# Add and GELU, 1024 x 4096 floats: another map from HBM rows to partitions

## The chip, the cores and the metric

The kernel runs on one core of one Trainium2 chip. The metric is the device time of the program in microseconds (us). A profiled execution gives a span, from the first to the last instruction, and its own device time, which is a little longer than the span.

## The reference

Two inputs of 1024 x 4096 float32 (16 MiB each), one output of the same size. Every element stands alone:

```python
def reference(x, y):
    z = x + y
    return (0.5 * z * (1 + np.tanh(np.sqrt(2 / np.pi) * (z + 0.044715 * z ** 3)))).astype(np.float32)
```

Since no element depends on another, any part of the flat arrays may sit in any partition, as long as x, y and the output use the same map.

## The kernel before

The 4,194,304 elements are dealt over 128 partitions, 32,768 to each (TOT), in two halves of 16,384 (HALF, 64 KB per partition). SBUF holds all of z (128 x 32,768, which receives x, then the sum, then the result) and one half of y, which is loaded twice into the same tile. One helper, `rows` (L91), says which bytes of HBM belong to columns lo to hi of all partitions; every load and store goes through it.

The transfers are few and large. SyncE issues all seven in this order (the list `sp`): y's columns 0 to 703 and 704 to 16,383 of the first half (`load_y`, L144), both halves of x (`load_x`, L139), the second half of y (L144), and the two halves of the output (`store`, L148). The first two issues are moved to the front of the program by `begin_early`; the last store's completion is waited for by ScalarE instead of SyncE (`wait_late`).

The compute is cut into 20 chunks of 512 to 2048 columns. A chunk is added on VectorE or on GpSimd (`add`, L159), in eight chunks with x copied to PSUM by ScalarE before (`copy`, L152), and then ScalarE applies the GELU in place (`gelu`, L171). Three lists written out by hand (`on_vector`, `on_gpsimd`, `on_scalar`) give each engine its order.

What waits for what: the adds of a half wait for both loads of it; y's second half is loaded into the tile of the first, so its issue waits until the first half's adds are through; a store waits for the GELUs of its half. All seven transfers run on one queue, spread over 16 DMA engines, in order of issue. A DMA engine moves one contiguous piece of one partition as one packet: 64 KB, or 2,816 and 62,720 B for the two pieces of y's first half.

Before the change, `rows` cuts the flat array into two blocks of 8 MB, one for each half, and deals each block to the 128 partitions in 64 KB rows: partition p has the row at p x 64 KB. Eight neighbouring partitions are 512 KB, and groups of eight follow each other at 512 KB.

## Time and profile before

| what | value |
|---|---|
| median of 3 runs | 120.17 us (120.12 to 120.42) |
| profiled execution | 120.31 us |
| its span | 118.8 us |
| DVE, ACT, POOL busy | 29.1, 44.1, 13.8 us |
| DMA packets | 1008, 50.33 MB |
| mean rate over the span | 424 GB/s |

The page gives shares of the span and groups of instructions; the DMA issues have a line each with the time from issue to landing. A landing counts from the issue, so it holds the wait behind earlier transfers of the same queue too. The trace also has a record for every DMA packet, with its start, its duration and its size. Of the 1008 packets 896 carry data, seven times 128; the other 112 are the few bytes that tell a semaphore that an engine is through with its part of a transfer.

### The profile page before, as it was taken

To read this page: it belongs to the slowest core of one execution; us is meant where nothing else is said; L and a number is where in the kernel's file an instruction comes from. 1 tells how busy PE (TensorE), PEld (TensorE's weight loads), DVE (VectorE), ACT (ScalarE), POOL (GpSimd) and SP (SyncE) were. 2 spreads that over 40 slices of the span, in tenths; PEclk is the share of its full clock that TensorE was granted. 3 is DMA by queue.
4 is the path that set the end of the run, shared out by engine and by line. 5 is a ranking of instruction groups with operands and counts; after the bars stand their busy time and mean duration, and the time that the engine had idled before them with its cause. 6 is when DMAs were issued, how large, how long until landed. Compare 5 with 4: busy or idle time off the path is not lost.

```text
span 118.8 us, 115 instructions
## 1 busy us (share of the span) xinstructions
DVE 29.1 (24%) x18; ACT 44.1 (37%) x30; POOL 13.8 (12%) x7
## 2 busy tenths in 40 slices
DVE  0000000000000099994000000009999930000000
ACT  4000000000000096893049999903799990000000
POOL 0000000000000019980000000009500000000000
DMA  9779977998889988998899888998899888988891
GB/s 459 338 338 422 591 338 338 507 552 353 353 353 662 397 353 353 574 485 353 353 441 618 353 353 353 640 419 353 353 552 507 353 353 353 706 353 353 353 640 66
DMA packets 1008, 50.33 MB, mean 424 GB/s; under 512 B 112, under 2 KB 112, under 8 KB 240
## 3 DMA queue, kind: packets, MB, share of 16 engines
q1 hardware_dynamic: 1008, 50.33, 98.5%
HBM read 33.55 MB, written 16.78 MB: 424 GB/s over the span
## 4 chain that ended last, share of the span: by engine, by line
DMA 55%; DVE 14%; ACT 10%; DVEq 1%; ACTq 0%; issue 0%; SPq 0%
DMA z<-in_x_dram 34%; DMA y<-in_y_dram 21%; DVE z L159 14%; ACT z L171 10%; DVEq L214 1%; ACTq L214 0%; DVEq L159 0%; SPq L144 0%
## 5 line engine op out<-in xcount | busy, mean ns | idle before, releaser
L171 ACT ACTIVATE z<-z 128x2048 f32<-128x2048 f32 (+3 forms) x20 | 29.7, 1555 | 5.4 <-DVE z L159 5.4
L152 ACT COPY ps<-z 128x2048 f32<-128x2048 f32 (+2 forms) x8 | 13.0, 1654 | 47.0 <-DMA z<-in_x_dram 45.3
L159 DVE TENSOR_TENSOR z<-z,y 128x2048 f32<-128x2048 f32 (+2 forms) x9 | 13.6, 1571 | 40.2 <-DMA z<-in_x_dram 40.2
L159 DVE TENSOR_TENSOR z<-ps,y 128x2048 f32<-128x2048 f32 (+2 forms) x8 | 15.6, 2014 | 25.3 <-DMA y<-in_y_dram 25.3
L159 POOL TENSOR_TENSOR z<-z,y 128x2048 f32<-128x2048 f32 x3 | 13.5, 4533 | 70.8 <-DVE z L159 43.6
L199 ACT ACT_TABLE_LOAD x1 | 1.3, 1283 | 1.3 <-PEq L231 1.3
L198 DVE MEMSET one<- 128x1 f32 x1 | 0.1, 59 | 1.3 <-PEq L231 1.3
L199 ACT ACTIVATE one<-one 128x1 f32<-128x1 f32 x1 | 0.2, 202 | 0.0
L231 POOL MEMSET const-float32-0.0<- 128x1 f32 x1 | 0.1, 99 | 0.2 <-issue 0.2
L231 POOL MEMSET const-bfloat16-1.0<- 128x1 bf16 x1 | 0.1, 102 | 0.0
L231 POOL MEMSET const-uint8-127<- 128x1 uint8 x1 | 0.1, 102 | 0.0
L231 POOL MEMSET const-float32-1.0<- 128x1 f32 x1 | 0.1, 99 | 0.0
## 6 DMA issues: line engine op xcount, KB each, us to landing
y<-in_y_dram SPq DMA_DIRECT2D x1, 7840.0 KB, 21.7
y<-in_y_dram SPq DMA_DIRECT2D x1, 352.0 KB, 3.0
z<-in_x_dram SPq DMA_DIRECT2D x2, 49.7
out_dram<-z SPq DMA_DIRECT2D x2, 21.6
y<-in_y_dram SPq DMA_DIRECT2D x1, 25.1
```

What stands on the lines that cost most here:

```text
L152: nc.scalar.copy(out=in_psum(c), in_=zt[:, a:b])
L159: ins = eng.tensor_add(out=zt[:, a:b], in0=first, in1=yt[:, o : o + b - a])
L171: nc.scalar.activation(out=zt[:, a:b], in_=zt[:, a:b], func=act.Gelu_apprx_tanh)
L198: nc.vector.memset(one[:, :1], 0.0)
L199: nc.scalar.activation(out=one[:, :1], in_=one[:, :1], func=act.Gelu_apprx_tanh)
L214: tc.compile()
L231: nc = _bacc.Bacc("TRN2", target_bir_lowering=False, num_devices=1)
```

## The change

`rows` takes another map. The flat array is cut into 16 parts of 1 MB (`q`). Each part is cut into two halves of 512 KB (`h`), and each of these into eight rows of 64 KB (`j`). Partition 8 q + j has, for half h, row j of half h of part q. So a group of eight partitions still has 512 KB in one piece for each half, but the groups lie 1 MB apart, and the two halves of the data alternate in HBM every 512 KB instead of filling 8 MB each. The view of the HBM side that a transfer gets has two counts (16, 8) and the columns instead of one count (128) and the columns; the SBUF side is not touched. Nothing else is changed.

```diff
-    blocks = [(0, HALF), (HALF, TOT)]
+    Q = 16
 
     def rows(array, lo, hi):
-        flat, at = array.rearrange("n d -> (n d)"), 0
-        for f, e in blocks:
-            if f <= lo and hi <= e:
-                own = flat[P * at : P * (at + e - f)].rearrange("(p c) -> p c", p=P)
-                return own[:, lo - f : hi - f]
-            at += e - f
-        raise AssertionError((lo, hi))
+        h = lo // HALF
+        assert hi <= (h + 1) * HALF
+        own = array.rearrange("n d -> (n d)").rearrange("(q h j c) -> h q j c", q=Q, h=2, j=P // Q)
+        return own[h][:, :, lo - h * HALF : hi - h * HALF]
```

## The prediction

> **What bounds the kernel now.** I read the page first, then the chain of waits, then SyncE's own waits, then the records of the single DMA packets. From the page, the busy time of the engines, the DMA queue and the DMA issues:

> ```profile
> span 118.8 us, 115 instructions
> DVE 29.1 (24%) x18; ACT 44.1 (37%) x30; POOL 13.8 (12%) x7
> q1 hardware_dynamic: 1008, 50.33, 98.5%
> HBM read 33.55 MB, written 16.78 MB: 424 GB/s over the span
> ...
> y<-in_y_dram SPq DMA_DIRECT2D x1, 7840.0 KB, 21.7
> y<-in_y_dram SPq DMA_DIRECT2D x1, 352.0 KB, 3.0
> z<-in_x_dram SPq DMA_DIRECT2D x2, 49.7
> out_dram<-z SPq DMA_DIRECT2D x2, 21.6
> y<-in_y_dram SPq DMA_DIRECT2D x1, 25.1
> ```

> No compute engine is busy for more than 37% of the span, and the one DMA queue fills its 16 engines for 98.5% of it: the kernel is a train of transfers. The chain that ended last, in order of time:

> ```profile
> 1.25 40.22 DMA z<-in_x_dram
> ...
> 41.60 13.36 DVE z L159 x7
> 54.96 0.02 SPq L144
> ...
> 55.02 25.12 DMA y<-in_y_dram
> ...
> 84.85 11.86 ACT z L171 x7
> ```

> It names DVE and ACT too, but the DMA engines work on meanwhile: the load of y's second half is issued at 55.02 while x's second half is still moving. SyncE's own waits say who holds an issue back:

> ```profile
> SPq L144 <- DVE z L159: 52.0, 1, 52.0
> SPq L148 <- ACT z L171: 41.9, 2, 21.9
> ```

> These waits cost little as long as an issue comes before the engines run dry, so I compared issues with packets. The trace holds 896 data packets, seven times 128 (one for each partition and transfer). Grouped by transfer (us from the span's start; ns of one packet; excess is the time above the fastest packet, per engine):

> ```
> transfer          issue   first packet  last ends   min   mean   max  excess
> y cols 0-703       0.00       1.03         2.63      109  151.5   769   340
> y cols 704-16383   0.42       2.25        21.84     2314 2371.7  2593   461
> x half 0           1.25      21.20        41.16     2418 2418.3  2422     2
> x half 1           1.63      40.54        60.48     2418 2418.8  2432     6
> y half 1          55.02      59.87        79.80     2418 2418.3  2431     3
> out half 0        77.33      79.20        99.11     2418 2418.0  2420     0
> out half 1        97.77      98.63       118.43     2418 2420.0  2456    16
> ```

> A 65,536 B packet takes 2,418 ns, 27.1 GB/s on one engine, and does so almost without exception in x, in the second y half and in both stores, reads and writes alike. That is the pace of a DMA engine alone with its packets, not that of a crowded memory. Time above it is paid in the first 22 us only: the small first packets (up to 769 ns against 109) and the long y rows, whose mean by row within an engine runs 2408, 2329, 2365, 2429, 2464, 2350, 2315, 2314 ns. In the course of that load the starts of the 16 engines' packets spread from 0.38 to 0.64 us, and from then on they keep to 2,418 ns. I read this as streams that begin nearly in step, get in each other's way, and push one another apart until they no longer do.

> The floor follows. Per engine 8 x 0.109 + 8 x 2.314 + 40 x 2.418 = 116.1 us of packets at their fastest; with the first packet at 1.03 us and 0.4 us from the last packet's end (118.43) to the span's end it is 117.5 us. The remaining 1.3 us are the excess above (0.340 + 0.461 + 0.03 = 0.83 us per engine) and 0.5 us from engines that start late (between 1.03 and 1.56 us).

> **The change part by part.** No instruction is added or removed and none moves past another: seven DMA issues, 18 DVE, 30 ACT and 7 POOL instructions stay, in the same order, with the same waits. Every partition still holds 16,384 consecutive values of each half; only which 64 KB of HBM they are differs, and reads and the store use the same map, so the arithmetic is the same. Compute and the waits in the table: 0.

> *Bytes and packets.* In the code the last dimension stays contiguous, 65,536 B (2,816 and 62,720 B for y's first half). Seven times 128 packets stay, sum 0.

> *The issue.* The HBM side is now described with two counts (16 and 8) instead of one (128). An issue takes SyncE 328 to 424 ns now (L144), and two of them lie open: the first, which nothing covers (the second y issue follows it, but its first packet waits for the 352 KB ahead of it until 2.25 us), and out half 1, issued at 97.77 where the first engine runs dry at 98.52 and the next packet starts at 98.63, so 0.11 us of idle are there already. The others are early by at least 1.9 us (out half 0: 77.33 against 79.20), the two x issues by 20 and 39 us. The trace shows no issue with two counts. Bounds: 0, and the spread of the issues that are there, 0.1 us, for each of the two, 0.2 us together. I take 0.05 us, near nothing, since the number of packets that has to be written is unchanged.

> *The addresses.* This is the change. If an engine takes eight neighbouring partitions, 16 streams which stood 512 KB apart, all 8 MB in a row, now stand 1 MB apart over the whole 16 MB. In the settled 97 us (x half 0 to out half 1, 40 packets an engine) the price of an address is at most 16 ns per eight packets. With the fastest packets already equal to the mean, nothing can be gained there. In the first 22 us between 0 and all of the 0.80 us excess can be gained (0.340 + 0.461), or it can grow. Bound above: if it doubles, +0.80 us. If the worst row of the y load (2464 against 2314 ns, 6.5%) held for all 48 long packets of an engine, 48 x 2.4 x 0.065 = +7.5 us. I take 0: the settled rows, which are nine tenths of the train, are the nearest, and whether a start in step at 1 MB apart collides more or less than at 512 KB no row tells.

> [...]

> **Sum.** 118.8 + 0.05 + 0 = 118.85 us of span. The profiled run took 120.31 us, 1.51 around its span, and lies 0.14 above the median of 120.17. Against the median: 120.2 us, no change. A difference of 0.3% (0.36 us) is about what a measurement of this kernel can tell from none.

> **Rivals.**

> *The start collides less (faster).* For: the only excess in the train stands there, it depends on which addresses are touched together, and spacing is what changes. Against: the small packets' excess may be the first access after a pause (the first of each engine averages 374 ns, the second 159, the third 119), which no address cures. Half of the 0.80 us, with the 0.5 us of late starts untouched, gives 119.8; all of it 119.4. I name 119.6.

> *The start collides more (slower).* The mechanism: all 16 streams begin within half a microsecond of each other at addresses that differ only in bits above 1 MB instead of 512 KB; if fewer of them tell the memory's parts apart, more streams meet, and they need longer to spread. Place: the y load in the first 22 us, perhaps once more in the first row of out half 1, where eight engines start together (2434 ns). Price: the excess doubles, +0.8, so 121.0. It decides from +0.36 us, that is when the mean y packet rises above 2,417 ns (2,371.7 + 360/8). For: row five of that load is worse than row one, so the streams do not simply drift apart. Against: from 17 us on (row seven) they are clear of each other.

> *The streams never clear (much slower).* Same place, but the collisions stay for all 48 long packets: 127.7 at the worst row's 6.5%. Against it stands that equal streams, once apart, keep their distance, as they do for 97 us now. [...]

> *The split over the engines changes.* SBUF still counts 128 partitions, HBM now 16 x 8. If the two are dealt to the engines differently than before, so that two engines share what one had, or only eight engines get work, the six halves of 19.35 us (x half 0 lands at 41.45, out half 1 at 118.8, four steps between) double: about 235 us. For: no transfer of this form is in the trace. Against: both 128 and 16 deal evenly over 16 engines.

> **How the numbers follow.** No change (within 0.3%) 0.38, start better 0.28, start worse 0.22, never clear 0.08, split 0.04. The likeliest is 120.2 and its own range is 119.85 to 120.55. To leave out no more than 2 in 10 the range takes in both cases of the start: its low end is 119.2, since all of the excess and a part of the late starts is the most that can go; its high end is 122.0, an excess that more than triples at the start. The last two cases, 0.12 together, stay outside. A case near the bound can fall on its other side, so: faster 0.30, same 0.35, slower 0.35.

> **What would show it.** Right: x, y half 1 and out packets still at 2,418 ns, 128 for each transfer, first packet at 1.0 to 1.1 us, and the landings 19.35 us apart from 22 us on. Faster by the start: x half 0's first packet before 20.9 us (now 21.20), all else shifted by as much. Slower by the start: the same packet after 21.6 us. Never clear: packets above 2,418 ns in x and the stores, landings more than 19.4 us apart. A changed split: other packet counts at a time, DMA share far under 98%. The forecast is wrong most easily by the start, whose 0.8 us is more than twice the bound.

## The result, and the profile after

The changed kernel takes 238.22 us (median of 5 runs, 238.05 to 239.96) against 120.17 us before: a ratio of 1.9857, 95% interval 1.9781 to 1.9934. Its profiled execution took 238.05 us with a span of 236.5 us, 117.7 us more than before.

The page of the changed kernel: busy time, the DMA share and rate in 40 slices of the span, the queue, and the issues with their time to landing.

```profile
span 236.5 us, 115 instructions
DVE 29.1 (12%) x18; ACT 44.1 (19%) x30; POOL 13.7 (6%) x7
...
DMA  9897889988889988889988889985989889998993
GB/s 231 170 339 170 170 170 203 321 177 177 177 177 211 321 177 177 177 177 244 288 177 177 177 177 266 266 177 211 321 177 355 177 177 244 199 244 222 211 211 89
...
q1 hardware_dynamic: 1008, 50.33, 98.8%
HBM read 33.55 MB, written 16.78 MB: 213 GB/s over the span
...
y<-in_y_dram SPq DMA_DIRECT2D x1, 7840.0 KB, 42.1
y<-in_y_dram SPq DMA_DIRECT2D x1, 352.0 KB, 4.0
z<-in_x_dram SPq DMA_DIRECT2D x2, 101.3
out_dram<-z SPq DMA_DIRECT2D x2, 56.4
y<-in_y_dram SPq DMA_DIRECT2D x1, 67.4
```

The same instructions are busy for the same time, the same 1008 packets move the same bytes, and the 16 DMA engines are as full as before, 98.8% against 98.5%. Only the rate is halved, 213 GB/s against 424. "Busy" counts a packet from its start to its end, whether it takes 2,418 or 5,070 ns for the same 65,536 B. The times from issue to landing of the large transfers grow by factors of 1.9 to 2.7; they hold the wait behind earlier transfers too.

The longest waits of the changed kernel (engine and line, what it waited for, total us, times, longest):

```profile
ACT ps L149 <- DMA z<-in_x_dram: 107.5, 2, 79.8
...
DVE z L156 <- DMA z<-in_x_dram: 81.3, 1, 81.3
...
DVE z L156 <- DMA y<-in_y_dram: 67.5, 1, 67.5
```

They are the old waits (45.3, 40.2 and 25.3 us before), stretched, and no new one. The packet records name the place. Grouped as in the prediction, x half 1 left out (us; ns of one packet; the mean of the eight rows that an engine moves, in order of start):

```
transfer          first packet  last ends   min   mean   max  rows 1 to 8
y cols 704-16383       2.70        41.95    4379  4842.7  4925  4629 4893 4894 4909 4704 4905 4906 4902
x half 0              41.20        82.45    4919  5070.9  5133  4922 5116 5123 5115 4927 5124 5121 5120
y half 1             122.20       163.44    4912  5069.4  5142  4917 5113 5115 5127 4928 5121 5115 5118
out half 0           162.68       198.00    2418  4302.0  5386
out half 1           196.88       236.19    2908  4672.8  5347
```

A packet that took 2,418 ns takes about 5,070 ns in the loads of x and of y half 1, and 4,302 and 4,673 ns in the mean in the two stores. The loads end at 163.44 instead of 79.80 us (+83.6), the stores add another 34.1. Two things can be read off. In the loads the slowness is there at the first long row and stays the same to the last: no start effect. And rows one and five of an engine are some 190 ns shorter than the rest in x and y half 1: something changes every four rows.

### The profile page after: what moved, and what is told of

Same layout as the page of the kernel before. It is cut to its first block, busy times and chain, and to the rows that moved or that the text cites. A ratio compares the mean times of both kernels' runs of the same rounds, so it can differ in the third digit from the quotient of the medians.

```text
span 236.5 us, 115 instructions
## 1 busy us (share of the span) xinstructions
DVE 29.1 (12%) x18; ACT 44.1 (19%) x30; POOL 13.7 (6%) x7
## 2 busy tenths in 40 slices
DMA packets 1008, 50.33 MB, mean 213 GB/s; under 512 B 112, under 2 KB 112, under 8 KB 240
## 3 DMA queue, kind: packets, MB, share of 16 engines
q1 hardware_dynamic: 1008, 50.33, 98.8%
HBM read 33.55 MB, written 16.78 MB: 213 GB/s over the span
## 4 chain that ended last, share of the span: by engine, by line
another core or an unknown queue 63%; DVE 7%; ACT 5%; DVEq 1%; ACTq 0%; issue 0%
DVE z L156 7%; ACT z L168 5%; DVEq L211 1%; ACTq L211 0%; DVEq L156 0%; DVE one L195 0%
## 6 DMA issues: line engine op xcount, KB each, us to landing
y<-in_y_dram SPq DMA_DIRECT2D x1, 7840.0 KB, 42.1
y<-in_y_dram SPq DMA_DIRECT2D x1, 352.0 KB, 4.0
```

## The experiments

Three theories. *Ports*: suppose that some partitions share a way into SBUF, that engines on one way at the same time share its pace, and that with two counts on the HBM side an engine gets eight neighbouring partitions, so that the 16 engines stand on half of the ways. Which partitions share, and how many ways there are, is supposed here; the pairs below have what the runs show of it. A packet's record in the trace names no partition, so which engine gets which partitions is inferred throughout. *HBM spacing*: streams 1 MB apart collide in HBM. *Form*: a transfer with two counts is slow in itself. Times are medians with the kernel before at 120.1 to 120.2 us beside them; all but the first experiment are single runs. Each lies further from the kernel before than that kernel's own runs lie from each other (0.4%). Of each edit the lines that carry it are shown.

### One count, the same 1 MB

```diff
-        own = array.rearrange("n d -> (n d)").rearrange("(q h j c) -> h q j c", q=Q, h=2, j=P // Q)
-        return own[h][:, :, lo - h * HALF : hi - h * HALF]
+        own = array.rearrange("n d -> (n d)").rearrange("(p h c) -> h p c", p=P, h=2)
+        return own[h][:, lo - h * HALF : hi - h * HALF]
```

> Each partition takes 128 KB in one piece, one half after the other, so groups of eight partitions lie 1 MB apart as in the changed kernel, but the HBM side has one count (128), as before the change. Ports theory (with two counts an engine gets eight neighbouring partitions, and two engines share one way into SBUF; with one count they are spread): 120 us, packets of 65,536 B at 2,418 ns. HBM spacing theory (streams 1 MB apart collide): near 238 us, packets near 5,100 ns. Form theory (a transfer with two counts is slow in itself, whichever partitions it goes to): 120 us.

Measured: 120.16 us, ratio to before 0.9996 (0.9981 to 1.0011). From its page:

```profile
span 118.7 us, 115 instructions
...
HBM read 33.55 MB, written 16.78 MB: 424 GB/s over the span
```

Groups of eight partitions at 1 MB cost nothing with one count. This does not yet rule HBM spacing out: no record tells which partitions an engine gets with one count, so the 16 streams of one moment may stand closer than 1 MB here. The y load's excess fell from 461 to 52 ns per engine, so a start can collide less, but the other transfers gave as much back (y half 1 went from 3 to 123 ns).

### Two counts, groups 64 KB apart

```diff
-        own = array.rearrange("n d -> (n d)").rearrange("(q h j c) -> h q j c", q=Q, h=2, j=P // Q)
+        own = array.rearrange("n d -> (n d)").rearrange("(h j q c) -> h q j c", q=Q, h=2, j=P // Q)
```

> Partition 8 q + j has row 16 j + q of its half: two counts (16, 8) as in the changed kernel, but the 16 groups lie only 64 KB apart and the eight rows of a group 1 MB. Ports theory: 238 us, packets near 5,100 ns, with the fourth and eighth row boundary visible as before. HBM spacing theory: the streams of one moment lie in one piece of 1 MB, so near 120 us. Form theory: 238 us.

Measured: 238.34 us, x packets 5,067 ns in the mean, with rows one and five at 4,885 and 4,901. Groups 64 KB apart instead of 1 MB, and the same time within 0.2 us: streams 1 MB apart are not what is slow. Ports and form stand.

### Half of the partitions at a time

In the kernel before, for `load_x` and likewise for `load_y` and `store`:

```diff
-        nc.sync.dma_start(out=zt[:, a:b], in_=rows(x, a, b))
+        for s in (0, 64):
+            nc.sync.dma_start(out=zt[s : s + 64, a:b], in_=rows(x, a, b)[s : s + 64])
```

> The kernel before with its own addresses and one count, each transfer cut in two of 64 partitions (0 to 63, then 64 to 127), so 14 transfers. Ports theory: the 16 engines work on half of SBUF's partitions at a time, so on half of its ways in, packets near 5,000 ns and about 235 us. HBM spacing theory: addresses in one piece as before, about 120 us, packets at 2,418 ns. Form theory: 120 us.

Measured: 239.13 us, x packets 5,068 ns. No second count anywhere, the addresses of before, and the loss is there: it does not need the form. Whether two counts are slow in themselves as well, the step-four runs below settle.

### The changed map with one count, an eighth at a time

In the changed kernel, for `load_x` and likewise for `load_y` and `store`:

```diff
-        nc.sync.dma_start(out=zt[:, a:b], in_=rows(x, a, b))
+        for j in range(8):
+            nc.sync.dma_start(out=zt[j:128:8, a:b], in_=rows(x, a, b)[:, j])
```

> The changed kernel's map, each transfer cut in eight: transfer j carries row j of all 16 groups, 16 rows 1 MB apart to 16 partitions eight apart, one count (16) on both sides, 56 transfers. Every engine has one row of each. Ports theory: at any time the 16 partitions in work are 8 e + j, the same ones as in the changed kernel, so about 236 us and packets near 5,000 ns. HBM spacing theory: the same addresses as in the changed kernel at the same time, about 236 us. Form theory (two counts are slow in themselves): no transfer has two counts, packets at 2,418 ns and 120 to 125 us.

Measured: 242.09 us, x packets 5,044 ns, rows one and five again the short ones (4,862 and 4,859). Giving every engine by hand the partitions 8 e + j, which the ports theory claims for the changed kernel, reproduces its x packets row by row, within 2%. The other 4 us are the eight times as many small y transfers (long y rows start at 6.9 instead of 2.7 us).

### Sixteen neighbours at a time

In the kernel before, for all three kinds of transfer:

```diff
-        nc.sync.dma_start(out=zt[:, a:b], in_=rows(x, a, b))
+        for s in range(0, P, 16):
+            nc.sync.dma_start(out=zt[s : s + 16, a:b], in_=rows(x, a, b)[s : s + 16])
```

> The kernel before with its own addresses and one count, each transfer cut in eight of 16 neighbouring partitions. Ports theory, with four partitions in a row and those 32 further on sharing one way into SBUF: the 16 engines share four ways, four engines on each, so packets near 4 x 2,418 = 9,700 ns and about 460 us, twice the changed kernel. If the loss were a fixed doubling of whatever is not a transfer of 128 with one count, it would be 240 us again. HBM spacing: 120 us.

Measured: 379.08 us. The loads did what was expected: every packet of x and of y half 1 takes 9,387 to 9,393 ns, 3.9 times 2,418, and the loads end at 302.1 us. The time is a miss, and the stores are why: 41.9 and 33.3 us for the two halves instead of some 75. Three stretches of this execution: x half 0 loading, then the first and the second store. Columns: stretch, length, busy us of DVE, ACT and POOL with instructions, PE clock, DMA share, GB/s.

```profile
80.00:150.00 70.00, 0.00 (x0) 0.00 (x0) 0.00 (x0) 1.00 0.94 105
305.00:340.00 35.00, 14.24 (x9) 14.38 (x10) 3.10 (x1) 1.00 0.91 180
343.00:370.00 27.00, 0.00 (x0) 0.00 (x0) 0.00 (x0) 1.00 0.82 262
```

The load keeps to a quarter of 424 GB/s; the stores gain pace as they go on. I read this as engines that push each other apart while they store, until they stand on different ways; in these loads they do not.

This run also parts SBUF from HBM. Here, and in the run with groups 64 KB apart if its engines hold eight neighbours each, the 16 engines read 16 rows of one piece of 1 MB at a time. With neighbouring partitions a packet takes 9,388 ns, with partitions eight apart 5,067, and with partitions eight apart and rows 1 MB apart (the experiment with an eighth at a time) 5,044. The time follows the partitions, not the addresses.

### Four engines ahead

```diff
+    def ahead(i):
+        nc.sync.dma_start(out=zt[4 + i : 32 : 8, HALF:TOT], in_=rows(x, HALF, TOT)[0:4, 4 + i, :])
+
-    sp = [(load_y, 0), (load_y, 1), (load_x, 0), (load_x, 1), (load_y, 2)]
+    sp = [(ahead, i) for i in range(4)] + [(load_y, 0), (load_y, 1), (load_x, 0), (load_x, 1), (load_y, 2)]
```

> The changed kernel, with four small transfers in front: each brings one row of x's second half (loaded again later) to four partitions, 4 + i + 8 e for engines e = 0 to 3, so that these engines begin y four rows, about 10 us, later than engines 4 to 7, which would share their ways into SBUF otherwise. 16 rows are loaded twice. Ports theory: engines 0 to 7 work on different groups of four partitions from then on, so half of the packets of x's first half take about 2,418 ns and half about 5,100; the time stays near 238 to 242 us, since engines 8 to 15 have not been helped. HBM spacing or form theory: nearly all packets of x's first half stay near 5,100 ns.

Measured: 237.79 us, and no fast half: every packet of x half 0 takes 4,787 ns or more. The third and fourth of the early rows were themselves slowed, to 5,048 to 5,074 ns, once the other twelve engines had begun with y, though by the ports theory nobody else was on their ways. Either the theory is wrong or a crowded way also slows engines that do not use it. The next three experiments tell these apart.

### Pairs, alone

```diff
+    groups = [...]
+
+    def ahead(i):
+        first, stop, step = groups[i]
+        nc.sync.dma_start(out=zt[first:stop:step, HALF:TOT], in_=rows(x, HALF, TOT)[first:stop:step, :])
+
+    def hold(i):
+        nc.sync.dma_start(out=yt[0:2, :], in_=rows(y, 0, HALF)[0:2, :])
```

`groups` holds four loads of each kind; all of them and `hold` go ahead of the first y load, in the kernel before.

> The kernel before, with 24 small loads ahead of it that run alone (y's first load waits for the last of them): rows of x's second half, loaded again later, two at a time to partitions 4, 64, 32, 1 and 8 apart (four loads each, two DMA engines), then four neighbours at a time (four loads, four engines). Ports theory, with p to p + 3 and p + 32 to p + 35 on one way into SBUF: pairs 4, 64 and 8 apart near 2,418 ns per packet, pairs 32 and 1 apart near 4,900 to 5,100, four neighbours near 9,400. A limit on eight-partition groups instead would make pairs 4 apart slow (8 to 11 and 12 to 15 lie across such a border, 48 to 51 and 56 to 59 in two) and pairs 32 apart fast. If only crowds of 16 engines are slow, all pairs are at 2,418.

The extra loads make the total, 212.72 us, mean nothing. The packet records of the stretch ahead, ns of each of the two engines' four packets, in order:

```
partitions      first engine            second engine
4 apart         3421 2422 2418 2418     2634 2418 2418 2418
64 apart        2418 2418 2418 2418     2418 2418 2418 2418
32 apart        4200 4986 4987 4986     4251 4987 4988 4987
1 apart         4595 5008 4549 5114     4702 5008 4785 5115
8 apart         2751 2418 2418 2418     2681 2422 2418 2418
```

This is the ports theory in its plainest form, with two engines only: partitions 4, 8 and 64 apart take nothing from each other once the first row is through, 32 or 1 apart they take half. (From the second load 1 apart to the third load 8 apart, two further engines were at the four-neighbour loads already, so the loads 32 apart are the clean ones. The distance in HBM goes along with the partitions here, 64 KB for each; the sixteen neighbours have parted the two. The four-neighbour loads never ran with four engines at once, so the 9,400 ns have no answer here, and rest on the sixteen neighbours.)

### Beside y's load

Small loads of this kind without `hold`, so that y goes on beside them: once six loads of four neighbours (0 to 3, 4 to 7 and so on), once six of partitions four apart (0, 4, 8, 12, then 1 and 2 on, and 16, 20, 24, 28, then 17 and 18 on).

> The kernel before, with six small loads of four neighbouring partitions each ahead of it, and nothing waits for them but x's second half: four engines load to one way into SBUF, while the other twelve go on to y. If a crowded way slows only those who use it, the four engines' packets take about 9,400 ns, and the packets of the other twelve in y stay near 2,314 ns but for the few rows that go to the same way (partitions 0 to 3 and 32 to 35 first). If writers held up by one way hold up others too, as four engines with a way of their own seemed to be in the experiment with four engines ahead, most y packets of the other twelve are well above 2,400 ns in the first 30 us.

> The same as the experiment with four neighbours beside y's load, but each small load goes to partitions four apart (0, 4, 8, 12 and so on), four ways. Ports theory: the four engines stay between 2,418 and about 5,000 ns, faster than beside with neighbours, and the other twelve's y packets near 2,314 ns or up to 5,000 where two engines meet on a way.

Measured with neighbours: the y packets of the other twelve engines that start between 5 and 15 us take 4,960 to 5,614 ns, all 24 of them. The 12 that start next, near 17 us, take 2,593 to 2,635 ns, and those between 19 and 40 us 3,796 to 7,702, while the small loads go on to 47.6 us. The small loads themselves take 2,720 to 9,129 ns and not 9,400 throughout: these four engines do come apart, on to different loads. With partitions four apart, in time:

```
starts at      small loads (ns)            y packets of the others (ns)
5 to 9 us      2418 (third load)           2412 to 2702
10 to 20 us    5056 to 5093                4684 to 4889, all 27
25 to 30 us    (done)                      2314 to 2341, all 34
```

While the small loads went to partitions 0 to 14, nobody was slowed; from the fourth load on (16 to 30) everybody was, although by the ports theory four engines on four ways can meet only some of the twelve there. When the small loads were through, the y packets were back at 2,314 ns at once. So, if the ports theory holds, a crowd on some ways can slow loads on others, though the 12 quick packets near 17 us show that it does not always. That would explain why shifting four engines did not help; it does not say where in the path they hang together.

### Loads alone, stores alone

A second helper `rows1` with the map of before serves the stores in one kernel, the loads in the other:

```diff
+    def rows1(array, lo, hi):
+        h = lo // HALF
+        own = array.rearrange("n d -> (n d)").rearrange("(h p c) -> h p c", h=2, p=P)
+        return own[h][:, lo - h * HALF : hi - h * HALF]
```

> The loads of x and y as in the changed kernel, the two stores with one count and the addresses of before (so the output holds its rows in another order than the reference). Ports theory: loads end near 163 us as in the changed kernel, stores at 2,418 ns per packet from their first row, 120.2 + 83.6 = about 204 us. If the stores were slowed by what the loads left behind, and not by their own dealing, their packets would stay above 2,418 ns.

> The loads with one count and the addresses of before, the two stores as in the changed kernel (so the output holds its rows in another order than the reference). Ports theory: loads end near 79.8 us as before, the stores take 73 us instead of 38.6, about 155 us in all. If the first two rows of a store are again at 2,418 ns, their pace has nothing to do with loads that were slow before them.

Measured: 204.26 us with slow loads, 159.76 us with slow stores. In the first, the stores are back at 2,418 ns after the first row (2,621): each side pays for its own dealing. The two losses, 84.2 and 39.7 us against the runs beside them, add up to 123.8, 5.8 more than the 118.0 that the change cost. 4.6 of these lie in the first two rows of out half 0: in the changed kernel they average 2,611 and 2,418 ns, with stores alone 4,574 and 5,034. Of these two kernels only the one with slow loads has the short first rows; why, no run shows.

### Step four, with one count and with two

Two kernels that cut each transfer in four of the same 32 partitions (j, j + 4, ... j + 124). The first on the kernel before, so with one count (32); the second on the changed map, so with two (16, 2). `load_x` is shown; `load_y` and `store` are cut likewise:

```diff
-        nc.sync.dma_start(out=zt[:, a:b], in_=rows(x, a, b))
+        for j in range(4):
+            nc.sync.dma_start(out=zt[j:P:4, a:b], in_=rows(x, a, b)[j:P:4])
```

```diff
-        nc.sync.dma_start(out=zt[:, a:b], in_=rows(x, a, b))
+        for j in range(4):
+            nc.sync.dma_start(out=zt[j:P:4, a:b], in_=rows(x, a, b)[:, j::4])
```

> The kernel before with its own addresses and one count, each transfer cut in four of 32 partitions, four apart (j, j + 4, ... j + 124), so each covers all 16 ways into SBUF, twice. If one count of 32 is dealt out in neighbours (engine e has j + 8 e, then j + 8 e + 4), eight ways are in use at a time and it takes about 238 us with packets near 5,000 ns. If a single count is spread over the ways whatever its size, 120 to 124 us with packets at 2,418 ns.

> The changed kernel's map, each transfer cut in four of 32 partitions four apart, as in the experiment with step four, but with two counts (16, 2) on the HBM side where that one has one count (32): the same partitions in each transfer, 28 transfers in both. If it is the form that decides which partitions an engine gets (two counts: neighbours in the list, 8 e + j and 8 e + 4 + j; one count: by the way into SBUF), eight ways are in use at a time, packets near 5,000 ns and about 238 us, against 123.6 with one count. If the dealing does not depend on the form, 120 to 125 us, and what sets the changed kernel apart is still unknown.

Measured: 123.64 us with one count, 206.46 us with two. The issues with their landing, first with one count, then with two:

```profile
y<-in_y_dram SPq DMA_DIRECT2D x4, 1960.0 KB, 13.9
...
z<-in_x_dram SPq DMA_DIRECT2D x8, 37.4
out_dram<-z SPq DMA_DIRECT2D x8, 13.6
```

```profile
y<-in_y_dram SPq DMA_DIRECT2D x4, 1960.0 KB, 25.4
...
z<-in_x_dram SPq DMA_DIRECT2D x8, 75.9
out_dram<-z SPq DMA_DIRECT2D x8, 24.7
```

The same partitions in each transfer, as many transfers, and x packets at 2,419 ns with one count and 4,888 with two. The addresses differ too, but the runs above took them out. Nor are two counts slow in themselves: in the second store of the two-count kernel 123 of 128 packets take less than 2,450 ns. So the counts decide which partitions an engine gets: with one count the engines are spread over the ways (2,419 ns), with two they get neighbours in the list (4,888 ns); this is read from packet times, as no record names a partition. The issue records of the traces show that the edit reaches the SBUF side too: the destination of the y loads reads dst_num_elem=[128,1] before and [1,128] after the change, [32,1] and [1,32] in this pair.

The total of 206 us is a miss against 238, again by the stores. Four stretches with two counts, two of loads and two of stores (columns as above):

```profile
40.00:80.00 40.00, 0.00 (x0) 0.00 (x0) 0.00 (x0) 1.00 0.98 210
80.00:120.00 40.00, 13.35 (x7) 11.21 (x7) 9.03 (x2) 1.00 1.03 220
...
162.00:182.00 20.00, 14.48 (x9) 14.52 (x11) 3.24 (x1) 1.00 0.98 328
182.00:204.00 22.00, 0.00 (x0) 0.00 (x0) 0.00 (x0) 1.00 0.89 381
```

Loads stay at half rate to their end. The second store's packets are at 2,430 ns in the mean. By the ports theory an engine changes its way with every row here, so one row of lead clears a pair; in the changed kernel it takes four rows, and the stores get only part of the way (4,302 and 4,673 ns).

## Why the prediction was wrong

The forecast of 120.2 us fell, and with it the range of 119.2 to 122.0. The case that came true is the one that had 0.04: "The split over the engines changes", priced at about 235 us against 238.22 measured, and with the mechanism it names, "two engines share what one had", though it does not say what is shared. That 235 comes so near is in part luck: doubling was to add 77.4 us in the loads and 38.7 in the stores, and the loads added 83.6, the stores 34.1.

*The bound.* Right and incomplete. The kernel is a train of transfers, and the added 117.7 us are packets. But "That is the pace of a DMA engine alone with its packets" holds only while no two engines share a way: two on partitions 32 apart took 4,987 ns. Before, each engine had a way of its own, as the step-four pair of runs indicates (2,419 against 4,888 ns); the trace of one dealing, at full pace throughout, could not show that the dealing mattered.

*Instructions and packets.* Right: 0 each.

*The issue.* Undersized. An issue takes SyncE 536 to 660 ns instead of 328 to 434 (the third y issue 0.54 against 0.33 us), and the first packet starts at 1.44 instead of 1.03 us: 0.4 us at the one exposed issue (itself 660 instead of 372 ns), where I took 0.05 with a bound of 0.1. The second one was not exposed any more, since the engines never ran dry.

*The addresses.* The step that was argued longest took 0 for the spacing, and no run speaks against it: groups at 1 MB with one count cost nothing (0.9996), and with two counts groups at 1 MB and at 64 KB take the same (238.22 and 238.34 us). Sixteen streams 1 MB apart at full pace were not measured. That address bits tell parts of the memory apart, the mechanism of the rival with the slower start, no run shows. The start did collide less in the one-count kernel (the y load's excess was 52 instead of 461 ns), and the gain was too small to tell. Its "nine tenths of the train" are 40 of 48 long rows, rather eight tenths; nothing hangs on it.

*The split.* This is the step that failed. Under the addresses it stands as a mere condition, "If an engine takes eight neighbouring partitions", with no price. The condition was taken to hold for the kernel before as well, where the runs speak against it (x packets at 2,418 ns); by the packet times it is what the change makes true (5,071 ns). Among the rivals the argument against it was "both 128 and 16 deal evenly over 16 engines". Even dealing is not enough. Eight neighbours for each of 16 engines is perfectly even and, by the ports theory, puts two engines on every way in use: engines four apart hold partitions 32 apart, which the pairs show at 4,987 ns. I looked for a resource that would be short of engines; the one that ran short was on the other end of the transfer, on the SBUF side, whose description in the code the change does not touch. The diff did show it: the HBM side went from one count to two, "no transfer of this form is in the trace", and that should have weighed far more than 0.04 when the price is a factor of two.

*The signs.* "DMA share far under 98%" was named as what a changed split would look like. It was 98.8%, at 213 GB/s. A DMA engine whose packets take twice as long is as busy in the page as before (98.5%); the sign to name was the packet's duration or the GB/s. Packets above 2,418 ns in x and the stores did stand among the signs, but for the case "never clear".

## What to carry to other kernels

A DMA share near 100% says that engines are occupied, not that bytes flow (98.8% at 213 GB/s, 98.5% at 424): put the GB/s and the ns of one packet beside it. When an access pattern gains or loses a dimension on either side, ask again which partitions each engine gets, also on the side that the edit does not name; a transfer over all 128 partitions can still run at half the pace (x packets at 5,071 ns instead of 2,418). Where a row map is free to choose, keep it to a single count over all 128 partitions: the 1 MB groups cost nothing in that form (120.16 us).

## What the runs showed of the hardware that was not expected

Loads and stores behave differently when their engines slow each other. Loads that all have the same work stay in step for good (9,387 to 9,393 ns for 384 packets with sixteen neighbours at a time; 4,888 ns with step four and two counts, to the end); only the four small loads beside y came apart (2,720 to 9,129 ns). A few small loads can slow the loads of all other engines (4,684 to 4,889 ns for all 27 y packets beside the small loads, 2,314 to 2,341 right after). Stores drift apart: from 9.4 us loads to a mean of 3,204 ns in the second store with sixteen neighbours, and to 2,430 ns with step four and two counts. In the changed kernel the first two rows of the store that follows the slow loads take 2,611 and 2,418 ns though the rest does not; with quick loads before the same store they take 4,574 and 5,034. That stays open.
